# A decoder trunk on one core: the first three key and value blocks computed row by row, four adaLN pairs behind them

## The chip, the core and the metric

The kernel runs on one core of a Trainium2 chip. The core has TensorE (matrix multiply), VectorE, ScalarE, GpSimd and SyncE, which issues the transfers from memory. The metric is the device time of one execution in microseconds (us), and the median of the runs counts.

## The reference, cut to what matters

One state-space layer is followed by one attention layer. Between them, the residual stream x (256 positions, 2048 features) is normalized, scaled and shifted by vectors that come from the conditioning c (adaLN), and multiplied by one matrix into six sets of keys and values:

```python
kv_shift, kv_scale = jnp.split(c_act @ kv_mod_w + kv_mod_b, 2, axis=-1)
h_kv = modulate(rmsnorm(x, kv_norm_g), kv_shift, kv_scale)
kv = (h_kv @ w_kv).reshape(B_, L, 2 * N_BRANCH, N_KV, HEAD_DIM)
kc = compress_blocks(kv[:, :, 0], ...)
vc = compress_blocks(kv[:, :, 1], ...)
# then the attention layer, with its own adaLN:
shift, scale, gate = jnp.split(c_act @ mod_w[layer] + mod_b[layer], 3, axis=-1)
h = modulate(rmsnorm(x, norm_g[layer]), shift, scale)
```

All is in float32.

## The kernel before

Activations lie with features on the partitions: the normalized matrix `hkv` is 16 rows (k = 0 to 15) of 128 features by 256 positions. A projection makes one block of 128 output features: `project` (line 232) opens an accumulator in PSUM (tag "mm", three buffers), loads the block's weights in two halves of 512 KB (eight rows of k each, line 191), and adds up over the 16 rows. To keep float32 accuracy with the faster matmul type, every weight and every activation is split into a rounded high part and a low remainder. `split_w` (line 195) does this for four rows at a time: ScalarE copies the high part `hi` (line 203), VectorE subtracts it to get `lo` (line 204). Each row then takes three matmuls: hi by high activation, hi by low, lo by high (lines 228 to 230), so a block has 48 of them. The split buffers `hi` and `lo` are four each (`hring`).

All weights pass through one ring of eight buffers of 512 KB (`ring`, tag "raw"; called a tile below). SyncE issues the transfers one behind the other, in the order of the program, each as soon as a buffer is free.

An adaLN vector of 128 features is made in one of two ways. `pe_mod_pair` (line 150) makes two on TensorE: four tiles of weights, 64 small matmul instructions (line 158), a copy by ScalarE (line 161), four small sums (line 163), two additions by ScalarE (line 166); its PSUM buffer "mc" is a single one. `dve_mod` (line 138) makes one on VectorE: two tiles, each multiplied by the conditioning and summed (line 145). Where these go is written out by hand: `PLAN` is a list of strings, and each call of `fill()` (line 593) takes the next: "d" is one vector on VectorE, "m" a pair on TensorE, "c" a piece of the compression network (one tile), "q" a row of the later query projection.

The order around the change is as follows. The output projection of the first layer ends (line 765), x is updated on VectorE (line 767) and the sum of squares kept up (line 245). `rms_scale` (line 247) sums it over the partitions on TensorE (line 250), takes the square root on ScalarE (line 252) and the reciprocal on VectorE (line 253). A `fill()` at line 784 takes "mmmm": four pairs, which belong to the later attention layer's adaLN. `norm_mod` (line 256) then makes each of the 16 rows of `hkv` in three steps: multiply (VectorE, line 260), shift and round (ScalarE, line 262), low part (VectorE, line 263). Then come 24 blocks; blocks 0 to 7 feed the compression (`cmp_block`, line 808): ScalarE copies the accumulator out (line 810), VectorE adds position vectors (line 814). After each block the next string of `PLAN` is taken. The compression pieces start after block 4 and the query rows (`q_rows`, line 888), which need the vectors of the four pairs, after block 12.

Every engine works off its instructions in a fixed order. The framework works that order out when the program is built, by a timeline that it estimates, so an instruction can stand ahead of one that is written before it.

Of the kernel before, what the change touches and what calls it, by code (L numbers as in the profile page):

```python
# [8 lines left out]
F32 = mybir.dt.float32  # L9
# [8 lines left out]
L = 256  # L18
KT = 16
# [27 lines left out]
def spread(n, slots, a=0):  # L47
# [16 lines left out]
    "mmmm",  # L64
# [8 lines left out]
def trunk_kernel(ctx, tc, xT, crow, ccol, vec, m0n, mn, mt, w_ur, w_in, w_glu, w_out, w_kv, w_qr, w_q, w_g,  # L73
                 w_z, w_o, cw1, cw2, b2row, lam, lstep, bmat, cmat, dvec, outT):
    nc = tc.nc
# [9 lines left out]
    ps = ctx.enter_context(tc.tile_pool(name="ps", bufs=3, space=PSUM))  # L85
# [9 lines left out]
    def raw_tile(name="raw"):  # L95
        return ring.tile([128, 8, 128], F32, tag="raw", name=name)
# [98 lines left out]
    def split_w(r, n):  # L195

        out = []
        for h in range(0, n, 4):
            c = min(4, n - h)
            hi = hring.tile([128, 4, 128], F32R, tag="hi", name="hi")  # L200
            lo = hring.tile([128, 4, 128], F32R, tag="lo", name="lo")
            rr = r[:, h:h + c, :]
            nc.scalar.activation(hi[:, 0:c, :], rr, AF.Copy)  # L203
            nc.vector.tensor_sub(lo[:, 0:c, :], rr, hi[:, 0:c, :].bitcast(F32))  # L204
            out.append((hi, lo))
        return out
# [25 lines left out]
    def project(src, act):  # L232

        acc = ps.tile([128, L], F32, tag="mm", name="acc")
        for half in range(2):
            project_half(src, act, half, acc)
        return acc

    def add_square(tot, xk, k):
        if k == 0:  # L240
# [214 lines left out]
    for s in (2, 3, 0, 1):  # L455
# [19 lines left out]
        for x in range(4):  # L475
            for g2 in range(2):
                pr = slice(64 * g2, 64 * g2 + 64)
                for ql in range(2):
                    h = 2 * x + ql
                    o = 64 * g2 + 32 * ql  # L480
                    for r in range(2):
                        nc.tensor.matmul(kp[o:o + 32, x].rearrange("p b m -> p (b m)"),
                                         bb[r][pr, 32 * h:32 * h + 32], kc_[pr, 2 * h:2 * h + 2, r, :],
                                         start=(x == 0 and r == 0), stop=True, skip_group_check=True)
# [264 lines left out]
    for m in range(16):  # L749
        acc = project(w_glu[m], yhl)  # L750
# [13 lines left out]
    for m in range(16):  # L764
        acc = project(w_out[m], ghl)
# [17 lines left out]
    hkv = Act(["va", "vb"], "hkv")  # L783
# [3 lines left out]
    kk = pool.tile([128, 4, 2, 528], F32R, tag="ca", name="kk")  # L787
# [14 lines left out]
    fl = zk[:, 2048:3968].rearrange("p (h l a b) -> p h l a b", h=2, l=16, a=4)  # L802
    fhl = pool.tile([128, 4, 2, 16, 60], F32R, tag="ha", name="fhl")

    def kv_block(t):
        return project(w_kv[t], hkv)

    def cmp_block(e, i):
        acc = kv_block(4 * e + i)
# [145 lines left out]
    acc = ps.tile([128, L], F32, tag="mm", name="acc")  # L955
# [23 lines left out]
    for m in range(16):  # L979
        acc = qacc[m // 2][:, m % 2, :] if m < QN else project(w_q[m - QN], hq)  # L980
# [7 lines left out]
    for h in range(16):  # L988
# [54 lines left out]
        for br in range(3):  # L1043
# [7 lines left out]
            else:  # L1051
                t = tsb[br - 1]
# [13 lines left out]
    for m in range(16):  # L1066
        acc = project(w_o[m], qo)
# [100 lines left out]
```

## Time and profile before

| what | value |
|---|---|
| time, median of 3 runs | 1360.05 us (1359.97 to 1362.2) |
| the profiled execution | 1356.18 us, its span 1354.5 us |
| mean granted TensorE clock | 0.971 |
| TensorE matmul busy | 1267.1 us |
| VectorE busy | 1056.9 us |
| ScalarE busy | 688.1 us |
| read from memory | 324.79 MB, 243 GB/s over the span |

The profile is one execution. Its times count from the first instruction. "Busy" of an engine is the time in which it has an instruction under way; matmuls are pipelined, so a busy TensorE may still have room. The granted clock is a share of TensorE's full 2.4 GHz; 0.50 is 1.2 GHz. The distance from one matmul's start to the next tells its speed better than its duration.

### The profile page before, as it was taken

The numbers are of one execution on the slowest core, as the hardware profiler recorded it, in microseconds if no ns is written. First come the engines' busy times: TensorE is split into PE (matmuls) and PEld (weight loads), VectorE is DVE, ScalarE is ACT, GpSimd is POOL, SyncE is SP. The second block draws the span as 40 slices with busy tenths as digits, with TensorE's granted clock in tenths as the row PEclk, the third lists the DMA queues.
The fourth block names the chain that finished last, engine by engine and source line by source line (L and its number), as shares of the span: only waits on it lengthen the run. The fifth ranks groups of instructions, "written<-read, shape, count | busy, mean of one in ns | idle before, by whom it ended". The sixth has DMA issues, their size and how long they took to land.

```text
span 1354.5 us, 31620 instructions
## 1 busy us (share of the span) xinstructions
PE 1267.1 (94%) x12526; PEld 1203.9 (89%) x12526; DVE 1056.9 (78%) x2291; ACT 688.1 (51%) x1463; POOL 21.7 (2%) x47
## 2 busy tenths in 40 slices
PE   2799999999889999998999899999999999999995
PEld 1678888888789999997999899999999999999995
DVE  5999769799768787659997878777888777776665
ACT  3345543437435555445455445555555565555653
POOL 2000000000100000000000000000000000000001
PEclk9899998999899999997999999999999999999998
DMA  9799954545879899869998789876555444444541
GB/s 342 259 384 316 350 194 147 212 138 197 295 280 362 299 344 327 309 232 385 322 352 272 241 278 326 273 253 216 175 199 192 149 154 145 154 143 154 187 157 62
DMA packets 93253, 331.05 MB, mean 244 GB/s; under 512 B 12512, under 2 KB 12672, under 8 KB 92080
## 3 DMA queue, kind: packets, MB, share of 16 engines
q1 hardware_dynamic: 91792, 321.45, 67.8%
q0 software_dynamic: 1312, 7.58, 1.5%
q8 instruction: 98, 1.61, 0.5%
q14 instruction: 51, 0.42, 0.1%
HBM read 324.79 MB, written 4.19 MB: 243 GB/s over the span
## 4 chain that ended last, share of the span: by engine, by line
PE 62%; DMA 4%; DVE 3%; issue 1%; ACT 1%; DVEq 0%; ACTq 0%
PE acc L230 18%; PE acc L229 18%; PE acc L228 18%; DMA raw<-in_mt_dram 3%; PE s L1002 1%; DVE lo L204 1%; PE op L1053 1%; PE macc L158 1%; PE op L1050 1%; DMA raw<-in_w_kv_dram 1%; DVE raw L145 1%; PE op L1054 1%; PE cp L838 0%; PE qacc L915 0%; PE cp L839 0%
## 5 line engine op out<-in xcount | busy, mean ns | idle before, releaser
L203 ACT ACTIVATE hi<-raw 128x512 fp32r<-128x512 f32 x640 | 400.0, 630 | 450.7 <-PE acc L229 388.6
L204 DVE TENSOR_TENSOR lo<-raw,hi 128x512 fp32r<-128x512 f32 x640 | 433.2, 688 | 154.5 <-ACT hi L203 148.2
L229 PE MATMUL acc<-hq,hi 128*128 128x256 f32 x960 | 274.6, 286 | 0.0
L228 PE MATMUL acc<-hq,hi 128*128 128x256 f32 x960 | 273.1, 285 | 0.4 <-ACT hi L203 0.4
L230 PE MATMUL acc<-hq,lo 128*128 128x256 f32 x960 | 271.0, 284 | 1.5 <-DVE lo L204 1.3
L145 DVE SCALAR_TENSOR_TENSOR raw<-raw,ey 128x1024 f32<-128x1024 f32 x156 | 189.9, 1220 | 63.0 <-DMA raw<-in_mt_dram 57.3
L229 PEld LDWEIGHTS acc<-hq,hi 128*128 128x128 f32 x960 | 181.0, 189 | 3.7 <-issue 3.3
L230 PEld LDWEIGHTS acc<-hq,lo 128*128 128x128 f32 x960 | 180.4, 189 | 3.5 <-DVE lo L204 2.1
L228 PEld LDWEIGHTS acc<-hq,hi 128*128 128x128 f32 x960 | 181.0, 189 | 1.2 <-issue 0.7
L230 PE MATMUL acc<-h,lo 128*128 128x256 f32 x384 | 112.3, 294 | 9.4 <-DVE lo L204 9.3
L230 PE MATMUL acc<-hkv,lo 128*128 128x256 f32 x384 | 112.3, 293 | 4.5 <-DVE lo L204 4.3
L228 PE MATMUL acc<-hkv,hi 128*128 128x256 f32 x384 | 112.0, 292 | 0.9 <-ACT hi L203 0.9
L228 PE MATMUL acc<-h,hi 128*128 128x256 f32 x384 | 112.8, 294 | 0.0
L229 PE MATMUL acc<-hkv,hi 128*128 128x256 f32 x384 | 111.0, 289 | 0.0
L229 PE MATMUL acc<-h,hi 128*128 128x256 f32 x384 | 110.2, 287 | 0.0
L230 PEld LDWEIGHTS acc<-h,lo 128*128 128x128 f32 x384 | 74.5, 195 | 12.4 <-DVE lo L204 11.4
L230 PEld LDWEIGHTS acc<-hkv,lo 128*128 128x128 f32 x384 | 76.1, 198 | 6.1 <-DVE lo L204 5.8
L158 PE MATMUL macc<-mraw,cz 128*32 128x128 f32 x1600 | 56.5, 292 | 24.4 <-DMA mraw<-in_m0n_dram 19.8
L228 PEld LDWEIGHTS acc<-hkv,hi 128*128 128x128 f32 x384 | 76.4, 199 | 1.5 <-ACT hi L203 1.5
L228 PEld LDWEIGHTS acc<-h,hi 128*128 128x128 f32 x384 | 74.6, 194 | 2.9 <-issue 0.8
L229 PEld LDWEIGHTS acc<-hkv,hi 128*128 128x128 f32 x384 | 76.4, 199 | 0.0
L229 PEld LDWEIGHTS acc<-h,hi 128*128 128x128 f32 x384 | 74.7, 195 | 0.0
(339 smaller groups left out, 2808.3 us busy)
## 6 DMA issues: line engine op xcount, KB each, us to landing
raw<-in_mt_dram SPq DMA_DIRECT2D x156, 512.0 KB, 5.8
raw<-in_w_z_dram SPq DMA_DIRECT2D x96, 512.0 KB, 3.8
mraw<-in_m0n_dram SPq DMA_DIRECT2D x64, 512.0 KB, 8.0
raw<-in_w_in_dram SPq DMA_DIRECT2D x48, 512.0 KB, 5.3
raw<-in_w_kv_dram SPq DMA_DIRECT2D x48, 512.0 KB, 6.2
mraw<-in_mn_dram SPq DMA_DIRECT2D x36, 512.0 KB, 6.1
raw<-in_w_glu_dram SPq DMA_DIRECT2D x32, 512.0 KB, 6.6
raw<-in_w_out_dram SPq DMA_DIRECT2D x32, 512.0 KB, 5.9
```

Of the source, the lines that this page charges most:

```text
L145: nc.vector.scalar_tensor_tensor(out=rf, in0=rf, scalar=1.0, in1=cact[:, 1024 * e:1024 * e + 1024], op0=OP.mult, op1=OP.mult, accum_out=mo ...
L158: nc.tensor.matmul(acc[32 * j:32 * j + 32, 128 * e:128 * e + 128], cz[:, q, :], r[:, q % 8, :], start=(e == 0 and q < 4), stop=(q >= 12), ...
L203: nc.scalar.activation(hi[:, 0:c, :], rr, AF.Copy)
L204: nc.vector.tensor_sub(lo[:, 0:c, :], rr, hi[:, 0:c, :].bitcast(F32))
L228: nc.tensor.matmul(acc, hi[:, kk, :], act(0, k), start=(k == 0), stop=False)
L229: nc.tensor.matmul(acc, hi[:, kk, :], act(1, k), start=False, stop=False)
L230: nc.tensor.matmul(acc, lo[:, kk, :], act(0, k), start=False, stop=(k == KT - 1))
L1002: nc.tensor.matmul(sp, qo(a, h)[:, qs], kk[:, kv, b, o:o + w], start=(i == 0), stop=(i == 2))
L1050: nc.tensor.matmul(op_, vc[0:15, kv, :], tcm[0:15, :], start=True, stop=True)
L1053: nc.tensor.matmul(op_, vt[:, kv, br - 1, 0, :], t[:, 0:256], start=True, stop=False)
L1054: nc.tensor.matmul(op_[:, 128:256], vt[:, kv, br - 1, 1, :], t[:, 256:384], start=False, stop=True)
```

## The change

A new function `project_rows` makes several blocks at once. It opens one accumulator for each, loads the same half of each block's weights, splits four rows of every one of them, and then goes row by row: for each k the three matmuls of every block, now in the order hi by high, lo by high, hi by low. It is called once, for blocks 0, 1 and 2, behind the writing of `norm_mod`; `kv_block` hands out the finished accumulators. In `PLAN` the string "mmmm" becomes empty, and the four pairs stand in the strings behind blocks 2, 3, 4 and 5.

```diff
@@ -61,8 +61,8 @@
-    "mmmm",
-    "d", "d", "d", "d", "dcd", "dc", "cd", "dcd", "cd", "cd", "cd",
+    "",
+    "d", "d", "md", "md", "mdcd", "mdc", "cd", "dcd", "cd", "cd", "cd",
@@ -235,6 +235,25 @@
+    def project_rows(srcs, act):
+
+        accs = [ps.tile([128, L], F32, tag="mm", name="acc") for _ in srcs]
+        for half in range(2):
+            raws = []
+            for src in srcs:
+                r = raw_tile()
+                nc.sync.dma_start(r, src[:, 8 * half:8 * half + 8, :])
+                raws.append(r)
+            for h in (0, 4):
+                w = [split_w(r[:, h:h + 4, :], 4)[0] for r in raws]
+                for kk in range(4):
+                    k = 8 * half + h + kk
+                    for acc, (hi, lo) in zip(accs, w):
+                        nc.tensor.matmul(acc, hi[:, kk, :], act(0, k), start=(k == 0), stop=False)
+                        nc.tensor.matmul(acc, lo[:, kk, :], act(0, k), start=False, stop=False)
+                        nc.tensor.matmul(acc, hi[:, kk, :], act(1, k), start=False, stop=(k == KT - 1))
+        return accs
@@ -802,8 +821,10 @@
+    first = project_rows([w_kv[t] for t in range(3)], hkv)
+
     def kv_block(t):
-        return project(w_kv[t], hkv)
+        return first[t] if t < 3 else project(w_kv[t], hkv)
```

## Rows read from the trace of the kernel before

**Rows 1.** The page: busy time by engine, and the ending chain by engine.

```profile
PE 1267.1 (94%) x12526; PEld 1203.9 (89%) x12526; DVE 1056.9 (78%) x2291; ACT 688.1 (51%) x1463; POOL 21.7 (2%) x47
...
PE 62%; DMA 4%; DVE 3%; issue 1%; ACT 1%; DVEq 0%; ACTq 0%
```

**Rows 2.** Windows: span, busy us of five engines, granted clock, DMA share, GB/s.

```profile
610.00:612.00 2.00, 0.86 (x32) 0.59 (x24) 1.98 (x7) 1.22 (x4) 0.00 (x0) 1.00 0.99 311
...
614.00:616.00 2.00, 2.00 (x44) 1.61 (x36) 2.00 (x7) 1.36 (x3) 0.00 (x0) 0.50 1.05 352
...
622.00:624.00 2.00, 1.09 (x17) 0.61 (x17) 0.03 (x1) 0.69 (x2) 0.00 (x0) 0.50 1.04 422
...
626.00:628.00 2.00, 2.00 (x10) 2.00 (x11) 2.00 (x5) 1.26 (x5) 0.00 (x0) 0.50 1.03 412
...
634.00:636.00 2.00, 2.00 (x19) 2.00 (x19) 2.00 (x6) 1.31 (x3) 0.00 (x0) 1.00 1.00 383
```

**Rows 3.** The chain that ended last, in time order: start, duration, what.

```profile
605.41 1.88 PE macc L158 x64
...
608.47 1.75 DVE rstd L253
...
613.82 9.46 DMA raw<-in_w_kv_dram
```

**Rows 4.** Timeline of TensorE: start, duration, instruction, idle time before and releaser.

```profile
605.34 1.95 PE L158 MATMUL macc<-mraw,cz 128*32 128x128 f32 x64
607.23 0.70 PE L250 MATMUL rsum<-tot,ones 128*128 128x256 f32 x2
607.80 0.61 PE L163 MATMUL macc<-ones,msum 128*128 128x1 f32 x4
...
620.76 1.08 PE L158 MATMUL macc<-mraw,cz 128*32 128x128 f32 x16 [1.60 <-DMA mraw<-in_mn_dram]
...
623.99 0.58 PE L228 MATMUL acc<-hkv,hi 128*128 128x256 f32 x1 [0.86 <-ACT hi L203]
```

**Rows 5.** Timeline of VectorE in the same stretch.

```profile
606.42 0.43 DVE L245 TENSOR_TENSOR tot<-tot,sq 128x256 f32<-128x256 f32 x1 [0.48 <-ACT sq L244]
...
613.83 0.48 DVE L263 SCALAR_TENSOR_TENSOR hkv<-xn,modv,hkv 128x256 fp32r<-128x256 f32 x1
614.23 0.15 DVE L904 SCALAR_TENSOR_TENSOR scol<-modv,vecs 128x1 f32<-128x1 f32 x1
...
621.10 0.48 DVE L263 SCALAR_TENSOR_TENSOR hkv<-xn,modv,hkv 128x256 fp32r<-128x256 f32 x1
623.97 0.69 DVE L204 TENSOR_TENSOR lo<-raw,hi 128x512 fp32r<-128x512 f32 x1 [2.39 <-ACT hi L203]
```

**Rows 6.** Timeline of ScalarE: rows, first weight splits, evacuations of blocks 0 and 1.

```profile
610.78 0.91 ACT L262 ACTIVATE hkv<-xn,modv 128x256 fp32r<-128x256 f32 x2 [1.92 <-DVE xn L260]
...
623.31 1.15 ACT L203 ACTIVATE hi<-raw 128x512 fp32r<-128x512 f32 x2 [3.16 <-DMA raw<-in_w_kv_dram]
...
634.31 0.37 ACT L810 ACTIVATE zk<-acc 128x256 f32<-128x256 f32 x1
...
640.07 0.37 ACT L810 ACTIVATE zk<-acc 128x256 f32<-128x256 f32 x1
```

**Rows 7.** Timeline of the transfer queue: first issue, length of the run of issues.

```profile
613.82 1.17 SPq L191 DMA_DIRECT2D raw<-in_w_kv_dram  x2
...
655.39 1.47 SPq L191 DMA_DIRECT2D raw<-in_w_kv_dram  x2
```

**Rows 8.** Timeline of TensorE: matmuls of block 0 and the first of block 6.

```profile
626.05 0.56 PE L230 MATMUL acc<-hkv,lo 128*128 128x256 f32 x1
...
630.04 0.41 PE L230 MATMUL acc<-hkv,lo 128*128 128x256 f32 x1
630.25 0.41 PE L228 MATMUL acc<-hkv,hi 128*128 128x256 f32 x1
...
670.62 0.37 PE L228 MATMUL acc<-hkv,hi 128*128 128x256 f32 x1
```

## The prediction

> **What bounds the kernel now.** I read four views in this order. The page first: TensorE works in 94% of the span, and the chain that ended last runs on it for 62% [rows 1]. So a gain must come out of a place where TensorE waits or runs at its low clock. The table of 2 us windows shows such a place: between 608 and 630 us its busy time falls to about half of a window or its granted clock to 0.50, while DMA stands at a share of 1.0, over 400 GB/s [rows 2]. The chain in order of time says what ended last there: the end of the output projection (605.4), the sum of squares, the square root, the reciprocal, the first rows of the normalized matrix, then 9.46 us of one transfer, the first weights of keys and values, from 613.82 to 623.3 [rows 3]. The timelines of TensorE, VectorE, ScalarE and of the transfer queue give the pieces.
>
> What TensorE does there: four adaLN pairs, the first of them at 605.34 [rows 4]. The fourth waits for its own weights at 620.76, and the first key matmul stands at 623.99, though 13 of 16 rows were normalized by 621.5 [rows 4, 5]. ScalarE shows why nothing came earlier: its first weight split sat idle 3.16 us for the transfer, with the last three rows queued behind it [rows 6]. The weights are late because the 16 tiles of the four pairs (half of them still to load at 605) stand ahead of them in the ring of eight buffers: the queue could issue the first of them only at 613.82 [rows 7]. VectorE is the second bound: after 626 it is busy 2.00 of 2.00 us in these windows, as TensorE is [rows 2].
>
> **The window, before.** From 605.4 to the end of block 2. A block at full clock takes 640.07 - 634.31 = 5.76 us, the distance of two evacuations [rows 6], or 0.120 us for each of its 48 matmuls; block 1 ended at 640.1, so block 2 at 645.8. A pair is 64 small matmuls in 1.95 us and four sums in 0.61, together 2.56 [rows 4]. The work is 3 x 5.76 + 4 x 2.56 + 0.70 for the sum of squares = 28.2 us, and it took 645.8 - 605.4 = 40.4. So 12.2 us are lost to waits and low clock; no more is to be had here.
>
> **The window, after, TensorE alone.** *Start.* The sum of squares no longer stands behind a pair: it was ready at 606.85 and ran at 607.23 [rows 4, 5], 0.35 us earlier. The high half of row 0 was ready at about 611.3 [rows 6], so TensorE starts at 611.0. The cover that the pairs gave is gone: it now idles 5 us there, which costs nothing by itself, since the pairs' 10.2 us are only moved and are paid behind.
> *Pace.* A row costs VectorE 0.80 us (two operations, each 0.40 to the next start [rows 5]) and brings 9 matmuls, 9 x 0.120 = 1.08 us. VectorE also makes 12 low halves at 0.61 us (623.97 to the next at 624.58 [rows 5]); four of them fit into its idle time up to 608.47 [rows 3], since their weights now land by 604 and four buffers exist; eight stay, 4.9 us. VectorE's total is 16 x 0.80 + 4.9 = 17.7 us from 609.9, so it is done at 627.6. TensorE's total is 17.3.
> *Clock.* At the low clock matmuls stand 0.21 us apart [rows 8]; before, 21 ran so from 626.05 to 630.25, then it rose. Another 21 now cost 21 x 0.093 = 2.0 us.
> *Split buffers.* This is new. A group of four rows uses three of four pairs of split buffers at once, so at each of three group boundaries two splits can start only when the group's last row is under way. From the end of the last matmul on one buffer to the new low half lie 0.25 + 0.63 + 0.13 + 0.69 = 1.7 us (ScalarE's split and VectorE's subtraction in [rows 6, 5]; the two gaps are my estimate from 623.31 + 0.61 to 623.97); 9 matmuls, 1.07 us, cover part of it. Bounds: 0.5 us each if VectorE is free, 1.7 if a row stands before it; no gain is possible, because before the change a split runs three quarters of a block ahead. I take 1.0, as rows are queued on VectorE throughout: 3.0 us.
> *Sum.* 611.0 + 17.3 + 2.0 + 3.0 = 633.3; the four pairs behind add 10.2: 643.5 against 645.8. **TensorE gains 2.3 us**, between 0 (boundaries at 1.7) and 5.7 (no boundary loss, no low clock).
>
> **The transfers.** The moved pairs carry 16 tiles of 512 KB past the queue of the kv stage. Counting tiles from the first of the window, before and after need the same 46 up to the second half of block 6: 16 of pairs, 14 of blocks 0 to 6, 14 of the adaLN on VectorE, 2 of compression. Before, the last two of these were issued at 655.39 [rows 7], and block 6 starts at 670.62 [rows 8]: the ring ran well ahead. Eight are in the ring at 605 in both cases. Before, the pairs' tiles are used up at once, so DMA ran full from 608 on [rows 2]. After, the eight are six halves of weights and two adaLN tiles, and the weights come free slowly: the first half block's at about 607, two more at the end of row group 0 (near 617), one near 623, two near 628; the two adaLN tiles (VectorE is idle enough at 602 to 605) and two more free four. That makes 9 or 10 issued in 605 to 628, so 17 or so have landed by 632; before, it was about 25 (the twelve windows from 608 to 632, between 311 and 422 GB/s [rows 2], have a mean of 380; 24 us of it are 17.4 tiles, on top of eight). Seen from the queue this change throws 8 tiles x 1.28 us = 10 us of transfer time away (1.28 us is 524288 B at 410 GB/s, about the 412 of 626:628 [rows 2]), and it is paid from the ring's lead. From 632 on, 28 more until the first half of block 6's weights: 632 + 28 x 1.28 = 667.8, and 0.9 for its first split: block 6 starts at 668.7, **1.9 us before** the 670.62 of now. Bounds: 20 tiles by 632 gives 664.9, where TensorE's own 2.3 decides; 14 gives 672.5, 1.9 later than now.
>
> TensorE's 2.3 and the transfers' 1.9 nearly meet; the later one counts, and a queue that never falls below 410 GB/s is the best case, as a pair's four tiles hold half the ring until TensorE, in its fixed order, reaches them. I put 1 us on that. Sum: -1.9 + 0.9 = -1.0 us. Behind block 6 a block needs five tiles, 6.4 us, about what its matmuls and its compression piece take (5.76 and some for the piece), so no more lead is lost, and TensorE, busy in 94% of the span [rows 1], passes the difference on to the end. The profiled execution, 1356.18 with its span of 1354.5, would become 1355.2. The median of three is 1360.05, 3.9 above it with the same program; the prediction is made there: **1359.0**. About 0.2%, 2.7 us, is what a measurement of this kernel can tell from no change.
>
> **The skill.** The granted clock was 1.00 up to 612, then 0.50 in 614:616 after pairs with gaps between them, and 0.50 again from 622 to 630 [rows 2]. The Trainium skill, page "TensorE: Matmul & The Clock Gate", section "Loop structure matters more than you think", speaks against this change: it wants all K tiles of one output back to back, as an array that waits between bursts falls back to 1.2 GHz. This trace agrees with the fall (0.50 of 2.4 GHz in those windows). By that rule all 144 row matmuls would run slow; it is rival 4.
>
> **Rivals.** (1) *The transfers keep up* (20 tiles by 632, splits ahead): the gain is TensorE's, 4 to 5.7 us, 1355. For it: 12 us are lost now, and VectorE's wait from 621.5 to 624 goes too [rows 5]. Against it: the ring count.
> (2) *The pairs collide with the kv stage*, slower: only 14 or fewer tiles by 632, and each of blocks 3 to 5 carries 8 to 11 tiles, 10 to 14 us of transfer against 5.76 + 2.56 = 8.3 us of TensorE work and some compression. It decides once fewer than about 15 have landed; with 12, and a low clock after each wait, block 6 starts at 675 to 677: +4 to +6, 1365. For it: DMA already stands at 1.0 here.
> (3) *Splits queue behind the rows*: written after all 16 rows, the low halves of row group 1 wait for VectorE's last row, near 622.5. Then TensorE stands from 617.5 to 623, and the transfers are released 5 us later too: +5, 1365. Against it: a later-written operation on one column ran at 614.23 between two rows [rows 5], so the order does pull work forward. Here the change would not do what it says.
> (4) *The clock stays low* over all rows: 144 x 0.093 = 13.4 us, 2.0 of them in the sum: +10, 1370. Against it: at 0.213 us apart nine matmuls take 1.9 us a row, longer than VectorE's 1.1, so TensorE is dense and the clock rose here after such a stretch (0.50 at 626:628, 1.00 at 634:636 [rows 2]).
>
> **How the numbers follow.** The forecast 0.53 (of it 0.10 faster by over 2.7 us, 0.41 within, 0.02 slower), rival 1 0.22, rival 2 0.12, rival 3 0.10, rival 4 0.02, 0.01 unseen. Faster 0.32, same 0.42 (a little of rival 3), slower 0.26. The range goes from rival 1's better end, 1353.5, to rival 2's and 3's worse end, 1366.5; rival 4 and half of the tails are left out.
>
> **What would show it.** Right: first key matmul near 611, the three evacuations together near 633, pairs at 633 to 660, DMA well below 1.0 up to 628, block 6 near 669.5. Wrong: TensorE idle over 3 us inside the rows (rival 3); long waits for weights or for pair tiles in blocks 3 to 5 (rival 2); DMA not idle at 610 to 620 (rival 1).

## The result and the profile after

The changed kernel took 1369.65 us, median of 5 runs (1367.36 to 1374.72), against 1360.05 of the kernel before (5 runs, 1358.32 to 1362.2). The ratio is 1.0079, with an interval of 1.0058 to 1.0101: slower by about 10 us, and outside the range that was forecast.

The page of the changed kernel: span, busy time by engine, and the chain that ended last by engine.

```profile
span 1367.0 us, 31616 instructions
...
PE 1275.4 (93%) x12526; PEld 1206.4 (88%) x12526; DVE 1057.5 (77%) x2291; ACT 686.9 (50%) x1463; POOL 21.9 (2%) x47
...
PE 60%; DMA 6%; DVE 4%; issue 1%; ACT 0%; DVEq 0%
```

Against [rows 1], TensorE has two points less of the chain, and transfers and VectorE three more between them.

TensorE, ScalarE and VectorE have the same instructions in the same order in both kernels up to 605 us, SyncE up to 581 us. Yet the last ScalarE copy of `ghl`, in that common part, starts at 509.81 before and at 513.87 after. These 4.06 us are a difference between two executions and not the change's. So all shifts below are counted from this copy: the start in a run, minus the start before, minus the shift of this copy in the run. Timeline of ScalarE in the kernel before: this copy and the last square of the program.

```profile
509.81 0.40 ACT L220 ACTIVATE ghl<-sg 128x256 fp32r<-128x256 f32 x1
...
1340.34 0.42 ACT L244 ACTIVATE sq<-x 128x256 f32<-128x256 f32 x1 [4.79 <-DVE x L1068]
```

The same two in the changed kernel:

```profile
513.87 0.40 ACT L220 ACTIVATE ghl<-sg 128x256 fp32r<-128x256 f32 x1
...
1352.89 0.42 ACT L263 ACTIVATE sq<-x 128x256 f32<-128x256 f32 x1 [4.79 <-DVE x L1089]
```

The end moved by 12.55 - 4.06 = +8.5 us, which lies in the interval of the ratio (7.9 to 13.7 us). On the way there the shift changes sign: +4.1 at the first normalized row, -2.7 at the end of block 2, +3.0 at block 5, +8.7 at block 7, +10.4 at the first key block, +8.5 at the end. So there are two things to explain: the norm's late start, and 13 us from block 2 to the first key block, of which 5 are the work of the two pairs that come after block 2. (The order put the small matmuls of the other two, 128 of 256, before and among the rows.)

**The norm.** Timeline of VectorE in the changed kernel, from 606 us to the first rows, and two lines from between later rows:

```profile
606.42 1.23 DVE L145 SCALAR_TENSOR_TENSOR raw<-raw,ey 128x1024 f32<-128x1024 f32 x1 [0.20 <-DMA raw<-in_mt_dram]
...
609.86 1.23 DVE L145 SCALAR_TENSOR_TENSOR raw<-raw,ey 128x1024 f32<-128x1024 f32 x1 [1.00 <-DMA raw<-in_mt_dram]
...
611.61 0.48 DVE L786 SCALAR_TENSOR_TENSOR x<-acc,modv,x 128x256 f32<-128x256 f32 x1
612.39 1.23 DVE L145 SCALAR_TENSOR_TENSOR raw<-raw,ey 128x1024 f32<-128x1024 f32 x1 [0.30 <-DMA raw<-in_mt_dram]
...
614.15 0.42 DVE L264 TENSOR_TENSOR tot<-tot,sq 128x256 f32<-128x256 f32 x1
615.24 1.23 DVE L145 SCALAR_TENSOR_TENSOR raw<-raw,ey 128x1024 f32<-128x1024 f32 x1 [0.67 <-DMA raw<-in_mt_dram]
...
616.59 1.75 DVE L272 RECIPROCAL rstd<-rstd 128x256 f32<-128x256 f32 x1
...
618.37 1.67 DVE L279 SCALAR_TENSOR_TENSOR xn<-x,scol,rstd 128x256 f32<-128x256 f32 x4
...
625.12 1.23 DVE L145 SCALAR_TENSOR_TENSOR raw<-raw,ey 128x1024 f32<-128x1024 f32 x1 [1.44 <-DMA raw<-in_mt_dram]
...
627.86 1.22 DVE L145 SCALAR_TENSOR_TENSOR raw<-raw,ey 128x1024 f32<-128x1024 f32 x1
```

The last update of x on VectorE in the kernel before:

```profile
605.45 0.48 DVE L767 SCALAR_TENSOR_TENSOR x<-acc,modv,x 128x256 f32<-128x256 f32 x1 [4.12 <-PE acc L230]
```

The last square on ScalarE in the changed kernel:

```profile
612.12 0.42 ACT L263 ACTIVATE sq<-x 128x256 f32<-128x256 f32 x1 [1.27 <-DVE x L786]
```

Four adaLN multiplications (L145), two vectors, stand in this chain: two ahead of the last update of x, one ahead of its sum of squares, one ahead of the reciprocal. Each waits for its own tile. Before, none stood between the last update at 605.45 and the reciprocal at 608.47 [rows 3]. The Trainium skill, page "TensorE: Matmul & The Clock Gate", section "Architectural detail: the array is 16× 32×32, not 1× 128×128", says that the queues of ScalarE and VectorE are strictly first in, first out. The trace agrees: the last square was ready at 612.54, but VectorE added it at 614.15, behind the multiplication that had started at 612.39 and a split. Two more multiplications stand between the rows (625.12 and 627.86), so that ScalarE's part of the last row comes 8.5 us late where that of the first came 4.1 late.

**The blocks.** Timeline of ScalarE in the changed kernel: evacuations of blocks 0 to 2, the splits of block 5's weights and of block 6's first half, the evacuation of block 6.

```profile
645.83 0.38 ACT L831 ACTIVATE zk<-acc 128x256 f32<-128x256 f32 x1 [5.05 <-PE acc L255]
...
646.63 0.38 ACT L831 ACTIVATE zk<-acc 128x256 f32<-128x256 f32 x1
...
647.41 0.38 ACT L831 ACTIVATE zk<-acc 128x256 f32<-128x256 f32 x1
...
666.38 2.44 ACT L203 ACTIVATE hi<-raw 128x512 fp32r<-128x512 f32 x4 [4.35 <-DMA raw<-in_w_kv_dram]
...
677.92 1.14 ACT L203 ACTIVATE hi<-raw 128x512 fp32r<-128x512 f32 x2
...
688.99 0.36 ACT L831 ACTIVATE zk<-acc 128x256 f32<-128x256 f32 x1
```

Blocks 0 to 2 do end together, but in block 5 ScalarE sits 4.35 us without weights, and block 6 starts late (TensorE's timeline of the changed kernel), 10.4 us behind 670.62 [rows 8], of which 4.06 are not the change's:

```profile
667.06 0.39 PE L228 MATMUL acc<-hkv,hi 128*128 128x256 f32 x1 [2.23 <-ACT hi L203]
...
680.94 0.28 PE L860 MATMUL cp<-fhl,lo 128*128 128x60 f32 x1
681.05 0.47 PE L228 MATMUL acc<-hkv,hi 128*128 128x256 f32 x1
```

Block 6 did not wait for its own weights: their first half landed at 677.79. TensorE was still at a compression piece (L860); it had stood 2.23 us for the weights of block 5.

Windows of the changed kernel (columns as in [rows 2]). They run from where the output projection ended before, 605.4, to 632, and then the 35.8 us in which the prediction wanted 28 tiles, all moved by 4.06, and what follows.

```profile
609.46:636.06 26.60, 18.79 (x177) 15.20 (x176) 23.73 (x52) 11.71 (x27) 0.00 (x0) 0.81 0.74 243
636.06:671.86 35.80, 33.35 (x336) 29.95 (x337) 27.70 (x55) 15.09 (x32) 0.00 (x0) 0.95 0.90 318
671.86:690.00 18.14, 17.52 (x171) 17.01 (x170) 13.03 (x25) 7.48 (x16) 0.00 (x0) 0.91 0.99 376
```

In the first, transfers have a share of 0.74 and 243 GB/s, where they stood near 1.0 before [rows 2]: the queue stood for want of free buffers, as forecast. In the second they ran at 318 GB/s, not at the 410 of the sum. That is the term that failed; it is worked out below.

### The profile page after: what moved, and what is told of

Read it like the earlier page. It is cut to its first block, busy times and chain, and to the rows that moved or that the text cites. A ratio compares the mean times of both kernels' runs of the same rounds, so it can differ in the third digit from the quotient of the medians.

```text
span 1367.0 us, 31616 instructions
## 1 busy us (share of the span) xinstructions
PE 1275.4 (93%) x12526; PEld 1206.4 (88%) x12526; DVE 1057.5 (77%) x2291; ACT 686.9 (50%) x1463; POOL 21.9 (2%) x47
## 3 DMA queue, kind: packets, MB, share of 16 engines
q8 instruction: 98, 1.61, 0.5%
## 4 chain that ended last, share of the span: by engine, by line
PE 60%; DMA 6%; DVE 4%; issue 1%; ACT 0%; DVEq 0%
PE acc L230 17%; PE acc L229 17%; PE acc L228 17%; DMA raw<-in_mt_dram 5%; DVE raw L145 1%; DVE lo L204 1%; PE s L1023 1%; PE op L1074 1%; PE macc L158 1%; DMA mraw<-in_mn_dram 1%; PE op L1071 1%; PE op L1075 1%; PE cp L859 0%; PE cp L860 0%; PE cp L858 0%
## 5 line engine op out<-in xcount | busy, mean ns | idle before, releaser
L145 DVE SCALAR_TENSOR_TENSOR raw<-raw,ey 128x1024 f32<-128x1024 f32 x156 | 189.9, 1220 | 74.9 <-DMA raw<-in_mt_dram 69.3
L230 PE MATMUL acc<-h,lo 128*128 128x256 f32 x384 | 111.8, 292 | 11.6 <-DVE lo L204 11.4
L230 PE MATMUL acc<-hkv,lo 128*128 128x256 f32 x336 | 99.9, 297 | 6.3 <-DVE lo L204 6.2
L228 PE MATMUL acc<-hkv,hi 128*128 128x256 f32 x336 | 98.5, 293 | 2.2 <-ACT hi L203 2.2
L229 PE MATMUL acc<-hkv,hi 128*128 128x256 f32 x336 | 97.6, 291 | 0.0
L158 PE MATMUL macc<-mraw,cz 128*32 128x128 f32 x1600 | 60.8, 298 | 24.9 <-DMA mraw<-in_m0n_dram 19.5
L158 PEld LDWEIGHTS macc<-mraw,cz 128*32 128x32 f32 x1600 | 46.5, 119 | 34.1 <-issue 22.1
L230 PEld LDWEIGHTS acc<-hkv,lo 128*128 128x128 f32 x336 | 66.7, 199 | 9.3 <-DVE lo L204 8.5
L230 PE MATMUL acc<-ghl,lo 128*128 128x256 f32 x256 | 72.2, 283 | 1.3 <-DVE lo L204 1.3
```

The costliest lines, as they stand in the source:

```text
L145: nc.vector.scalar_tensor_tensor(out=rf, in0=rf, scalar=1.0, in1=cact[:, 1024 * e:1024 * e + 1024], op0=OP.mult, op1=OP.mult, accum_out=mo ...
L158: nc.tensor.matmul(acc[32 * j:32 * j + 32, 128 * e:128 * e + 128], cz[:, q, :], r[:, q % 8, :], start=(e == 0 and q < 4), stop=(q >= 12), ...
L228: nc.tensor.matmul(acc, hi[:, kk, :], act(0, k), start=(k == 0), stop=False)
L229: nc.tensor.matmul(acc, hi[:, kk, :], act(1, k), start=False, stop=False)
L230: nc.tensor.matmul(acc, lo[:, kk, :], act(0, k), start=False, stop=(k == KT - 1))
```

## The experiments

Four theories are named in the expectations. T: the moved pairs' tiles press on the weights of blocks 3 to 8, after a time in which the ring stood full. H: adaLN multiplications stand on VectorE ahead of work that others wait for, and wait there for their tiles (head of line). R: the row-by-row order itself costs. P: the pairs' work has lost its cover, the time in which TensorE waited for the norm anyway. Shifts in us, as defined above, one profiled execution each; ratios are to the kernel before, from runs beside it on the same chip.

| run | ratio (95%) | row 0 | block 2 | block 5 | block 7 | key 1 | key 4 | query | end |
|---|---|---|---|---|---|---|---|---|---|
| changed kernel | 1.0079 (1.0058 to 1.0101) | +4.1 | -2.7 | +3.0 | +8.7 | +10.4 | +10.6 | +7.2 | +8.5 |
| e1 moved pairs only | 1.0044 (1.0022 to 1.0066) | +7.7 | +2.5 | +8.4 | +11.2 | +11.3 | +14.9 | +7.7 | +8.5 |
| e2 rows only | 1.0040 (1.0020 to 1.0060) | +0.2 | -1.3 | +4.9 | +4.7 | +4.1 | +5.1 | +3.0 | +4.4 |
| e3 changed, no transfers | 1.0058 (1.0030 to 1.0085) | +7.6 | -1.4 | +0.8 | +0.7 | +1.1 | +3.5 | +6.4 | +5.9 |
| e4 before, no transfers | 1.0109 (1.0076 to 1.0143) | +12.4 | +0.6 | +1.6 | +2.8 | +4.4 | +11.7 | +11.7 | +11.2 |
| e5 changed, rows first | 1.0119 (1.0077 to 1.0161) | +0.8 | -13.2 | +7.1 | +14.1 | +14.4 | +14.4 | +14.5 | +15.5 |
| e6 before, no transfers, rows first | 1.0043 (1.0015 to 1.0070) | +0.6 | -3.9 | -4.5 | -3.0 | -1.2 | +0.4 | +4.2 | +4.7 |
| e7 changed, rows and splits first | 1.0029 (1.0008 to 1.0049) | +0.3 | -9.2 | +9.2 | +13.5 | +14.6 | +17.8 | +5.2 | +2.8 |
| e8 before, rows and splits first | 0.9956 (0.9937 to 0.9976) | +0.6 | -0.1 | +3.9 | +5.2 | +4.7 | +12.0 | -0.6 | -3.0 |
| e9 changed, rows first, no transfers | 1.0079 (1.0052 to 1.0107) | +1.8 | -6.2 | -2.5 | 0.0 | +2.6 | +13.8 | +11.5 | +11.4 |
| e10 pairs in the output projection | 1.0160 (1.0122 to 1.0198) | +13.7 | +9.0 | +11.9 | +19.0 | +21.5 | +29.8 | +29.9 | +29.3 |
| e11 before, late splits first | 0.9907 (0.9880 to 0.9934) | +0.9 | +1.3 | -0.2 | -0.2 | -0.2 | -0.2 | -11.3 | -13.7 |
| e12 as e10, with e5's and e11's constraints | 0.9989 (0.9966 to 1.0013) | +10.0 | -4.1 | +6.5 | +7.7 | +7.9 | +10.0 | -1.2 | -3.7 |
| e13 changed, late splits first | 0.9974 (0.9953 to 0.9994) | +4.2 | -0.9 | +4.1 | +8.9 | +9.8 | +11.4 | +0.4 | -2.0 |
| e14 rows only, late splits first | 0.9935 (0.9911 to 0.9958) | 0.0 | -2.4 | +2.3 | +2.1 | +1.5 | +1.9 | -9.4 | -11.8 |
| e15 moved pairs only, late splits first | 0.9957 (0.9939 to 0.9976) | +5.8 | -0.3 | +4.1 | +8.0 | +7.6 | +7.9 | -3.4 | -5.8 |
| e16 two pairs in front, late splits first | 0.9990 (0.9970 to 1.0011) | +4.4 | +7.0 | +8.2 | +12.6 | +12.9 | +12.9 | +1.6 | -0.8 |

"Row 0" is ScalarE's part of the first normalized row, "block N" the evacuation of a block. "Key 1" and "key 4" are the first evacuations of the first key block and the last of the fourth, "query" the first evacuation of a whole query block, "end" the last square.

How far one shift can be trusted, the table shows itself. Four pairs of builds (before and e11, changed and e13, e2 and e14, e1 and e15) have the same instructions in the same order on the compute engines up to at least 716 us, past the first key block. Up to there their shifts still differ by up to 1.3, 1.8, 2.6 and 4.3 us. So a difference of less than about 4 us between two shifts shows nothing by itself.

### The halves of the change, and the transfers taken away (e1 to e4)

e1 is the kernel before with the new `PLAN`; e2 is the changed kernel with the old one:

```diff
-    "mmmm",
-    "d", "d", "d", "d", "dcd", "dc", "cd", "dcd", "cd", "cd", "cd",
+    "",
+    "d", "d", "md", "md", "mdcd", "mdc", "cd", "dcd", "cd", "cd", "cd",
```

> The kernel before with only the four pairs moved behind blocks 2 to 5; blocks 0 to 2 stay block by block. Theory T (the moved pairs' 16 tiles collide with the transfers of the kv stage): the loss is there without the rows, 8 to 12 us slower than before, long waits for adaLN tiles in blocks 3 to 7. Theory R (the row order itself, its split buffers and what is pulled in front of it, costs the time): within 3 us of before. Theory P (only the pairs' 10.2 us of TensorE time have lost their cover): 3 to 6 us slower, without waits for transfers in blocks 3 to 7.

> The changed kernel with the four pairs back in front of the rows; the three blocks stay row by row. Theory T: within 3 us of before, since the first weights land near 623 again and all rows are ready by then. Theory R: 5 to 10 us slower than before. Theory P: as T.

In e3 (changed kernel) and e4 (kernel before) the four pairs read a matrix that is already in memory; their 16 tiles are not loaded, so their vectors are not computed from their weights:

```diff
-                if q % 8 == 0:
+                if q % 8 == 0 and npe[0] >= NA:
+                    r = cact[:, 0:1024].rearrange("p (a b) -> p a b", b=128)
+                elif q % 8 == 0:
```

> The changed kernel, but the four moved pairs multiply by a matrix that is already on the chip, so their 16 tiles are not loaded and the later adaLN vectors are not the reference's; all of TensorE's work is kept. Theory T: the loss goes, from 2 us slower to 6 us faster than before. Theory R and theory P: still 6 to 10 us slower than before.

> The kernel before, its four pairs without their 16 tiles in the same way (the later adaLN vectors are not the reference's). It is the measure for the one before: how much the tiles cost where they stand now. Theory T: the kv weights are there when the rows are, 6 to 10 us faster than before. If the tiles were hidden where they stand: within 3 us of before.

By their end times both halves cost some 0.4%: by the medians e1 4.8 us, which is P's range and less than T's (but P wanted no waits for transfers, and VectorE waits 5.7 us for adaLN tiles in e1 from 645 to 715), and e2 4.4 us, between the ranges of T and R. e3 came out 9 us slower than the kernel before, as R and P had it, and e4 13 us slower, which nothing had foreseen. At first I read this as the end of T. The shifts by stage say otherwise for e3: at the first key block it stands at +1.1 and the changed kernel at +10.4. But e3 does not take away the tiles alone. With no tile to wait for, the order put all four pairs before and among the rows, so their work had its cover again. From block 2 to the first key block the changed kernel loses 13.1 us, 5.1 of them the work of two pairs; e3 loses 2.5. So some 5.5 us of the difference are tiles, little more than one shift varies by itself, and the rest is cover. e3 gives 5 us back later.

e4 gave H. Timeline of VectorE in e4:

```profile
605.05 1.23 DVE L145 SCALAR_TENSOR_TENSOR raw<-raw,ey 128x1024 f32<-128x1024 f32 x1 [3.10 <-DMA raw<-in_mt_dram]
...
613.31 1.23 DVE L145 SCALAR_TENSOR_TENSOR raw<-raw,ey 128x1024 f32<-128x1024 f32 x1 [1.78 <-DMA raw<-in_mt_dram]
...
621.67 1.23 DVE L145 SCALAR_TENSOR_TENSOR raw<-raw,ey 128x1024 f32<-128x1024 f32 x1 [3.70 <-DMA raw<-in_mt_dram]
...
622.82 1.75 DVE L255 RECIPROCAL rstd<-rstd 128x256 f32<-128x256 f32 x1
```

Without the pairs' tiles ahead of them in the ring, adaLN multiplications were put ahead of the norm, and the reciprocal came at 622.82 instead of 608.47 [rows 3] (3.0 of these 14.4 us e4 had already at `ghl`). The pairs in front had kept that place closed: the first row stands at +0.2 and 0.0 with the pairs in front (e2, e14), at +7.7 and +5.8 with the pairs moved (e1, e15). Yet the late norm is not what made e4 slower in the end. By block 2 it was made up (+0.6); the loss came between block 7 (+2.8) and the fourth key block (+11.7), where VectorE again waited for adaLN tiles. Its waits in e4 from 686 to 738 (total us, times, longest; 0.6 us in all in the kernel before):

```profile
DVE raw L145 <- DMA raw<-in_mt_dram: 11.3, 6, 3.0
```

### The place ahead of the norm closed by hand (e5, e6)

```diff
+                with (tc.issue_after(anchor[0]) if anchor[0] is not None else nullcontext()):
-                nc.vector.scalar_tensor_tensor(out=rf, in0=rf, scalar=1.0, ...)
+                    nc.vector.scalar_tensor_tensor(out=rf, in0=rf, scalar=1.0, ...)
...
     norm_mod(x, rstd1, scol, modv[:, 96:112], hkv)
+    anchor[0], live[0] = last[0], True
```

`last[0]` is the last row's low half (the operation of line 263). This fixes an order; it adds no work.

> The changed kernel, with one constraint on the order: no adaLN multiplication of the keys-and-values stage stands on VectorE ahead of the last of the 16 normalized rows. All work and all transfers are the same. Theory H (head of line: such multiplications stand on VectorE ahead of the norm and of rows, wait there for their tiles, and everything behind them waits too): the first normalized row comes 4 to 5 us after the output projection's end (8.1 in the changed kernel, 4.9 before), no wait of VectorE for a tile inside the rows, and the time is 3 to 8 us below the changed kernel: ratio to the kernel before 0.998 to 1.005. Theory T (the moved pairs' tiles collide with the weights of blocks 3 to 5 on the transfers): the norm comes earlier but block 6 does not, ratio 1.006 to 1.010 as in the changed kernel. Theory R (the rows' own order and the four split buffers cost it): the evacuations of blocks 0 to 2 move by under 1 us against the changed kernel, ratio 1.006 to 1.010.

> The kernel before, whose four pairs use a matrix that is already in memory instead of their 16 tiles (part of the computation is left out: these four vectors are wrong), as in the earlier run of that, and now with the order constraint: no adaLN multiplication on VectorE ahead of the last normalized row. Theory H: the loss of 13 us that came with taking the transfers away was multiplications pulled ahead of the norm, waiting for their tiles; with the constraint the reciprocal comes 3 to 4 us after the output projection's end, and the time is at least 10 us below the earlier run: ratio to the kernel before 0.992 to 1.002. Against it (the loss has another cause, such as TensorE's clock after a gap or the memory's rate): ratio 1.007 or more.

e6 went H's way, if not all of it: 9 us less than e4 by the medians (1363.99 and 1373.11), the norm's start back at +0.6, the ratio between the two cases. e5 missed. The norm starts where it did before, yet the kernel is no faster for it: +15.5 at the end against +8.5, with intervals of the ratios that overlap. VectorE's timeline in e5:

```profile
610.86 1.75 DVE L279 RECIPROCAL rstd<-rstd 128x256 f32<-128x256 f32 x1 [1.30 <-ACT rstd L278]
```

ScalarE's timeline, the evacuations of blocks 0 to 2:

```profile
633.88 0.94 ACT L839 ACTIVATE zk<-acc 128x256 f32<-128x256 f32 x3 [4.94 <-PE acc L262]
```

The windows of e5:

```profile
606.00:612.00 6.00, 2.65 (x19) 2.04 (x17) 3.77 (x6) 2.15 (x4) 0.00 (x0) 0.99 0.28 91
612.00:618.00 6.00, 4.27 (x20) 4.27 (x21) 5.96 (x15) 3.48 (x8) 0.00 (x0) 0.50 0.02 6
618.00:624.00 6.00, 6.00 (x49) 6.00 (x49) 6.00 (x15) 4.57 (x11) 0.00 (x0) 0.94 0.18 48
624.00:630.00 6.00, 6.00 (x62) 5.67 (x61) 6.00 (x14) 3.40 (x7) 0.00 (x0) 1.00 0.42 145
630.00:636.00 6.00, 5.38 (x75) 4.98 (x78) 6.00 (x12) 0.94 (x3) 0.00 (x0) 1.00 1.00 332
636.00:642.00 6.00, 1.13 (x21) 0.78 (x13) 4.30 (x12) 1.54 (x5) 0.00 (x0) 0.77 1.02 394
```

All three blocks are evacuated from 633.88 on, the last of them 13.2 us earlier than block 2 was before. But from 606 to 630 the transfers moved (91 + 6 + 48 + 145) x 6 us = 1.74 MB, 3.3 tiles: the ring was full, with weights that TensorE had not used up and adaLN tiles that now waited behind the rows. At 636 to 642 TensorE works 1.13 of 6 us with the transfers at 1.02. This is what T describes: from block 2 (-13.2) to block 7 (+14.1) 17.1 us are lost beside the 10.2 us of the pairs' work. So the multiplications ahead of the norm are a trade. They cost the norm 4 us, and they free the buffers that keep the transfers running (from 606 to 630 on average 220 GB/s in the changed kernel, 73 in e5).

### e5 without the pairs' transfers (e9)

The edit is that of e5 and of e3 together.

> The run of the changed kernel with rows first, but the four moved pairs use a matrix that is already in memory instead of loading their 16 tiles (part of the computation is left out: these four vectors are wrong). The order on VectorE is held by the same constraint, so that it tells about transfers alone. Counted from the last point of equal work (near 510 us), the first key evacuation stood 14.4 us later than before in the run with rows first, though blocks 0 to 2 ended 13.1 us earlier. Theory T (the ring stands full while the norm runs, and the pairs' tiles then press on the weights of blocks 3 to 8): without these tiles the first key evacuation is 10 to 17 us earlier than in that run, shift -3 to +4; time 8 us or more below it, ratio to the kernel before at most 1.005. Theory H alone (the order, not the transfers): shift at the first key evacuation still 11 or more, ratio 1.009 or more.

One window of e9:

```profile
606.00:630.00 24.00, 22.66 (x294) 19.19 (x293) 20.04 (x44) 14.10 (x32) 0.00 (x0) 1.00 0.25 82
```

What VectorE waited for in e9 from 695 to 745 (total us, times, longest):

```profile
DVE raw L152 <- DMA raw<-in_mt_dram: 17.3, 5, 5.0
```

The ring stands as full as in e5 (82 GB/s up to 630), but the first key block is at +2.6 instead of +14.4: 11.8 us less with 16 tiles less. The constraint holds VectorE's order and not TensorE's: as in e3, the pairs ran before the end of block 2 (-6.2 there). From block 2 to the first key block e5 loses 27.6 us, 9.1 of them work of the pairs, and e9 8.8. So about 10 us are the tiles: T holds for blocks 3 to 8. The expected time was missed: from the first key block to the fourth 11 us are lost again while VectorE waits 17.3 us for adaLN tiles. That is the sign of H at another place; it was not tested there.

### The pairs inside the output projection (e10), and the constraints together (e7, e8, e11, e12)

```diff
-    "d", "m", "d", "", "d", "d", "", "m", "d", "", "d", "", "d", "", "", "",
+    "d", "m", "d", "", "d", "d", "", "m", "d", "m", "d", "m", "d", "m", "m", "",
```

> The changed kernel with the four pairs not behind blocks 2 to 5 but inside the output projection ahead of the norm, where the transfers have a share of only 0.45 to 0.55 of the time. Blocks 0 to 2 still go row by row. Theory T: the transfers no longer press on blocks 3 to 8, and what is left is the rows' own gain on TensorE, about 3 us (blocks 0 to 2 ended 13.1 us earlier in the run with rows first, the pairs take 10.2): ratio 0.995 to 1.002, first key evacuation at a shift of -4 to +3. Theory R (the row-by-row order itself costs in blocks 3 to 8, as all split buffers and three accumulators are taken until block 2 ends): shift +4 or more, ratio 1.004 or more. Theory H can add to either: multiplications that stand ahead of the norm show as a later first row.

A plain miss. What ScalarE waited for in e10, 540 to 760:

```profile
ACT hi L203 <- DMA raw<-in_w_out_dram: 16.1, 4, 6.6
```

Of the +13.7 at the first row, 10.2 are the pairs' own work, for which TensorE has no idle time there: it is busy in 64.78 of the 65 us from 540 to 605 before. The projection's own weights are late, too, but the last update of x stands at +11.8, so this cost at most 1.6 us by then. The rows then take 9.6 us longer than before. How the +29 (23 us by the medians) split up behind that was not told apart.

e7 and e8 hold, behind the rows, every adaLN multiplication behind the last weight split that is written before it; e11 does this from block 12 on and has no constraint on the rows:

```diff
-            nc.vector.tensor_sub(lo[:, 0:c, :], rr, hi[:, 0:c, :].bitcast(F32))
+            sub_ = nc.vector.tensor_sub(lo[:, 0:c, :], rr, hi[:, 0:c, :].bitcast(F32))
+            if live[0]:
+                anchor[0] = ins_of(sub_)
...
     for i in range(24):
+        if i == 12:
+            live[0] = True
```

> The changed kernel with the constraint of the run with rows first, and a second one: behind the rows, no adaLN multiplication of the stage stands on VectorE ahead of a weight split that is written before it. Theory H for blocks 4 to 8 (the same mechanism goes on there: multiplications wait for tiles with splits behind them): 2 to 6 us below the run with rows first, ratio 0.994 to 1.002. Theory T: no difference to the run with rows first (within 2 us), since the weights themselves are late. If multiplications run later, their tiles come free later too, and the ring feeds more slowly: then it is slower than the run with rows first by 2 us or more.

> The kernel before with both constraints. It tells whether the second constraint helps by itself: theory H says little is to be had here, as waits of VectorE for adaLN tiles are 5.9 us in all in this stage: ratio 0.996 to 1.001. If the constraint costs (tiles come free later), 1.002 or more, and then the run of the changed kernel with both is to be read against this one.

> The kernel before, with the constraint on adaLN multiplications behind weight splits only from block 12 on (in the run with both constraints from block 0, the trace lost 12 us up to the last of the first key blocks and won 12 from there to the query rows). Theory H: VectorE's 16.9 us of waits for adaLN tiles between 720 and 860 stand ahead of splits, and without them 6 to 13 us are won with no loss before: ratio 0.990 to 0.996. Rival: the won time was only the lost time given back (a ring that is ahead again), then 0.997 to 1.001.

In both kernels the second constraint loses between blocks 4 and 11 and wins some 12 us from there to the query, so e11 keeps its second half alone. e8 came out a little better than expected, e7 6 us further below e5 than expected, with a ratio of 1.0029 still just above its range. Windows of the kernel before:

```profile
740.00:760.00 20.00, 17.29 (x139) 16.48 (x138) 14.67 (x30) 9.82 (x21) 0.00 (x0) 1.00 0.69 233
760.00:780.00 20.00, 17.29 (x132) 17.09 (x132) 16.10 (x36) 9.29 (x20) 0.00 (x0) 0.91 0.75 250
```

Its waits of VectorE from 720 to 860:

```profile
DVE raw L145 <- DMA raw<-in_mt_dram: 16.9, 9, 3.9
```

The same windows of e11 (which stands 6.2 us later at `ghl`):

```profile
740.00:760.00 20.00, 20.00 (x170) 20.00 (x170) 17.92 (x34) 10.81 (x22) 0.00 (x0) 1.00 0.79 269
760.00:780.00 20.00, 19.99 (x166) 19.79 (x165) 19.69 (x45) 12.63 (x27) 0.00 (x0) 1.00 0.84 279
```

TensorE's idle time there is gone, and VectorE no longer waits for adaLN tiles in this stage. e11, 1348.61 us, is faster than both kernels: 0.9907. It has nothing to do with the change; it is H, found on the way.

> Search for a version that beats both: pairs inside the output projection, blocks 0 to 2 row by row, no adaLN multiplication of the stage ahead of the last normalized row, and from block 12 on none ahead of a weight split. Theories T and H together: the first row 4 to 5 us behind the output projection, 3 us from the rows and 6 to 10 from the late constraint: ratio 0.988 to 0.995, below the run of the kernel before with the late constraint. If the full ring during the rows (transfer share near 0.1 there) costs even without the pairs' tiles, block 4 to 8 wait for weights and the ratio is 0.997 or more.

e12's second case came: 0.9989. Its first row stands at +10.0, about the pairs' own 10.2 us again. Windows of e12:

```profile
620.00:630.00 10.00, 5.30 (x23) 4.90 (x24) 8.61 (x19) 4.59 (x11) 0.00 (x0) 0.72 0.40 161
630.00:640.00 10.00, 10.00 (x79) 9.85 (x78) 9.64 (x22) 6.64 (x14) 0.00 (x0) 0.94 0.33 105
640.00:650.00 10.00, 6.18 (x50) 5.77 (x48) 10.00 (x19) 4.29 (x10) 0.00 (x0) 0.91 0.81 276
650.00:660.00 10.00, 7.33 (x39) 7.34 (x40) 9.88 (x22) 1.77 (x3) 0.00 (x0) 0.57 0.94 334
```

The pairs' tiles are long gone, and still the transfers stand at 0.33 to 0.40 during the rows and TensorE starves behind them. So the rows stop the queue by themselves. By the program, three blocks' weights come free only when their splits find buffers, at the ends of the row groups; no run takes that apart from the rest.

### The halves again, with the late order held (e13 to e16)

The same late constraint on the changed kernel (e13), on e2 (e14), on e1 (e15), and on the changed kernel with "mm" in front and two pairs behind blocks 4 and 5 (e16).

> The changed kernel with the late constraint alone (from block 12 on no adaLN multiplication on VectorE ahead of a weight split). To be read against the kernel before with the same constraint (ratio 0.991 to the kernel before). If the change's cost stands in blocks 0 to 8 (transfers and the norm's start, 10 us in the trace at the first key evacuation): shift there +9 to +12, the constraint then wins 8 to 12 behind it as it did in the kernel before: ratio 0.997 to 1.002. If the cost stood in the order behind block 12: ratio 0.990 to 0.994.

> Blocks 0 to 2 row by row, but the four pairs in front as before, with the late constraint. Theory T: the pairs in front keep the transfers running, so little is lost: first key evacuation at a shift of 0 to +5 (+4.1 without the constraint), ratio 0.991 to 0.995. Theory R (the rows themselves cost): shift +8 or more, ratio 0.997 or more.

> Only the four pairs moved behind blocks 2 to 5, blocks 0 to 2 one by one as before, with the late constraint. Theories T and H put the whole cost here: first key evacuation at a shift of +9 to +13, ratio 0.997 to 1.003. If moving alone is harmless and only together with the rows it costs: shift 0 to +4, ratio 0.990 to 0.994.

> The changed kernel with two of the four pairs in front of the norm and two behind blocks 4 and 5, with the late constraint. Theory T (each pair moved behind brings 4 tiles past a queue that stood still during the rows): between the run with four in front and the one with four behind, shift at the first key evacuation +4 to +8, ratio 0.993 to 0.998. If the loss is all or nothing (multiplications ahead of the norm as soon as the front is open): shift +9 or more; if two in front are cover enough: +4 or less.

Against e11's end of -13.7, the rows alone cost 1.9 us (e14), the move alone 8.0 (e15), both 11.7 (e13); the medians are 1348.61, 1350.99, 1355.36 and 1356.76, so by them 2.4, 6.8 and 8.2. The move is the dear one. The cost of the rows alone is not clear of noise here: the intervals of e11 and e14 overlap, and the shifts differ by less than 4 us. In the order without the constraint it was (e2, 1.0040). e15 stands a little under what was expected (first key block +7.6 for +9 to +13, ratio 0.9957 for 0.997 to 1.003). e16 missed: two pairs in front are no better than none. The chain to the reciprocal is free of multiplications there, but eight of them, 1.2 us each, stand between the rows, and ScalarE's part of row 15 comes at +13.8; why the order was laid so was not followed further, so T's cost per pair is not shown.

## Why the prediction was wrong

- **TensorE's own gain: right for rows that start on time.** The sum had the three blocks end at 633.3, and -2.3 us after the pairs. e5 is nearly the case that was summed, with the norm on time: 633.88 - 1.58 (its shift at `ghl`) = 632.3, and -13.2 + 10.2 = -3.0. (The upper bound of 5.7 does not follow from its own words: without boundary loss and low clock the sum gives 7.3.) The clock too: 0.50 in 612:618, then 0.94 and 1.00 in e5's windows above, so rival 4 did not come. The Trainium skill, page "TensorE: Matmul & The Clock Gate", section "Loop structure matters more than you think", shows the K tiles of one output back to back as the good case and a wait for a transfer before every matmul as the bad one. Here three accumulators took turns, and the clock was granted all the same. In the changed kernel itself block 2 ended at -2.7 with 5.1 us of pairs' work still to do: +2.4 by the same count, not -2.3.
- **"Two adaLN tiles, VectorE is idle enough at 602 to 605": wrong.** Two vectors' multiplications were indeed pulled ahead, but they were not free. Their tiles had not landed, and they stood in the chain: +4.1 at the first row, +8.5 at the last. Rival 3's row at 614.23 [rows 5] had shown that the order pulls work forward; I used it as comfort and did not ask what it would pull into the place that the pairs left.
- **The count of tiles up to 632: near.** By the trace's landing times 19 of the 46 tiles had landed at 636.06 (632 moved by 4.06); I had 17. Before it was 23 at 632, not 25. So the change threw 4 tiles of lead away, not 8.
- **"28 x 1.28 us" from 632 on, with 1 us for the doubt: the step that failed.** The first half of block 6's weights is tile 45 of the 46. It landed at 677.79, so 26 tiles took 41.7 us, 1.61 us each; at 1.28 they would have taken 33.3. That is 8.4 us more, and the better count gave 2.6 back, so the weights came 5.9 us later than the forecast 667.8 + 4.06 = 671.9. Block 6 started 3.3 us behind them instead of 0.9, as TensorE was still busy with what the late weights of block 5 had held up. Together it started at 681.05 instead of 672.8, 8.3 us late.
- **Why a tile took longer.** The 410 GB/s came from the two best of five windows [rows 2], with the transfers at a share of 1.03 and 1.04. In the changed kernel the ring kept standing behind 632, too: from 652 to 664 the transfers' share was 0.70 to 0.88, and from 636 to 678 at most three tiles were under way in 37% of the time. In the kernel before, from 632 to 661.7, this was so in 4% of the time, and 22 tiles took 1.35 us each. So about 2 us of the 8.4 (0.07 us a tile) are the best windows' rate, which even the kernel before did not hold, and the rest is most likely waits for buffers; no run separates the two. A better price was on hand, the mean of the kernel before over this stage:

```profile
636.00:672.00 36.00, 35.08 (x282) 34.75 (x281) 34.79 (x67) 17.58 (x30) 0.00 (x0) 0.95 0.93 336
```

  At 336 GB/s a tile takes 1.56 us. With the forecast's 28 tiles block 6 would start at 676.6, 6.0 us late; it was 6.4 (10.43 - 4.06). That the two are so close is partly luck, as two tiles too many stand against the 2.4 us behind the landing.
- **Rival 2** (the pairs collide with the kv stage, 0.12) is what happened, later (from block 5 on) and dearer than its +4 to +6. Its condition, fewer than 15 tiles by 632, was not met (19): what the queue does behind that decides.
- **The rest of the way to the end** was to be passed on without further loss. The shift grew from +6.4 at the start of block 6 to +10.4 at the first key block and came back to +8.5 at the end, 9.5 us above the forecast -1.0. Every edit also lays the order behind block 12 anew: from the fourth key block to the end the shift went down by 13.5 us in e11, by 6 in e1, by 2 in the changed kernel and hardly in e4, so an end time alone tells little of the stage that was edited.

What stays open: why the order puts multiplications where their tiles haven't landed (the times that it estimates are not on record), e16, the parts of e10, and which buffer the queue waited for behind 632. A ring of more buffers would be the direct test of T; it was not tried.

## What to carry to other kernels

A step in front of a stage can hold a place in the order. Before moving it, ask which instructions the order will pull into the gap, what they wait for, and who stands behind them on that engine. Cost a queue that has lost its lead at the mean rate of the stage that must make it up, waits for free buffers included, and not at its best window. When a step leaves a place where an engine was idle anyway, count its work again at the place it goes to. And compare builds by their shift from the last common instruction, stage by stage: end times mix a change with what the order does elsewhere. Then find out from builds with the same order how much such a shift varies by itself.

## What the runs showed beyond that

Taking 8 MB of transfers away made the kernel before slower by 1.1% (e4), as the order then put adaLN multiplications where they waited for their tiles; one constraint on the order gave 9 of the 13 us back (e6). And a constraint that adds no work took 0.9% off the kernel before (e11).
